# x ahead of the first scale block, low parts on VectorE, wider scale blocks: one transformer block on one core

## The chip, the core and the metric

The kernel runs on one core of a Trainium2 chip. A core has five engines, each with a queue of its own that it works through strictly in order: TensorE (PE in the profile, its weight loads PEld), VectorE (DVE), ScalarE (ACT), GpSimd (POOL) and SyncE (SP), which here issues most of the loads. An instruction waits for others by semaphores, and everything behind it on its engine waits with it. The metric is device time in microseconds (us) of one execution; lower is better.

## The reference

One decoder layer for 512 tokens of width 2048, in f32. What matters here is its head, and the MLP at its end:

```python
mod = (jax.nn.silu(c) @ w_ada[l] + b_ada[l])                 # 6 x 2048 values
shift1, scale1, gate1, shift2, scale2, gate2 = ...
h = rms_norm(x, norm1_w[l]) * (1.0 + scale1) + shift1
proj = h @ w_in[l]                                           # 2048 x 7168
...                                                          # attention, HGRN2, w_out, residual
h2 = rms_norm(x, norm2_w[l]) * (1.0 + scale2) + shift2
ff = jnp.square(jax.nn.relu(h2 @ w_ff1[l])) @ w_ff2[l]
x = x + gate2 * ff
```

## The kernel before

Every f32 product is computed as three fast ones: an operand is split into a high part, a cast (`hi`, `whi`, `vhi`), and a low part, the rest (`lo`, `wlo`, `vlo`), and TensorE adds high x high, high x low and low x high (`L205` to `L207` in the helper `ch_mm`). The casts run on ScalarE. The low parts of weights (`L40`) run on VectorE.

**The head.** scale1 is a product of one vector with 2048 columns of w_ada. It is not done on TensorE but by `gemv` on VectorE: for each of 16 row blocks k of w_ada a load (`araw`) and one instruction `acc = araw * sc[k] + acc` (`L127` for the first two, `L129` after), in two accumulators for even and odd k. `to_cols` then turns the sums over: TensorE transposes them (`pc`, `L149`), ScalarE adds them up along the rows (`L152`), and VectorE makes the scale columns `g1c` of them (`L167`, `L169`). A block of 256 columns of scale1 gives two columns of g1c, so it serves two row blocks k of the projection; it takes 32 instructions for 512 columns where a block of 512 takes 16 and one addition of the accumulators (`L143`).

x is loaded in 16 pieces (`xs`), squared and summed (ScalarE, VectorE), scaled by the reciprocal root, and transposed on TensorE (`ptx`) into 16 tiles `xnT[k]`. `scaled(k)` multiplies xnT[k] by g1c on ScalarE, casts `hi`, and takes `lo = xnT - hi` on GpSimd. `first_groups` runs the first 768 columns of w_in over k in pairs, six products of 128 columns with three matmuls each: 18 matmuls for one k. Before each pair of k it calls `scale_block`, which does the gemv of the next 256 columns of scale1. I call this the scale stage.

A second `first_groups` follows (the shift stage): 768 further columns with the same scaled operands, while VectorE does the gemv of shift1 (four blocks of 512), and `shifted(k)` adds the shift to hi and xnT and takes the low part on GpSimd. What the shift would have added to the columns of the first two groups is added later by another gemv over w_in (`shift_through`). Then comes a part whose TensorE order is written by hand (`project`, from `L197` on), up to the MLP.

**The border.** The second MLP product is a Strassen-like scheme of seven products (`product`, i = 1, 3, 5, 6, 7, 4, 2 at first) on halves of the weights: `part` forms a combination of raw weight tiles on VectorE where the product needs one (`L1073`, `L1077`), casts `vhi` on ScalarE and takes `vlo` on VectorE (`L1084`). There are four buffers for vhi and vlo. The product with `early` set is put at high priority; before, that is the first alone.

**What sets the order.** The program is written once, and a scheduler places each engine's instructions by a time line that it computes itself; `issue_after` and `high_priority` steer it. So an edit in one place can change the order of several engines, and the engine queues on the chip keep that order whatever the real times are.

Of the kernel before, what the change touches and what calls it, by code (L numbers as in the profile page):

```python
# [8 lines left out]
F32 = mybir.dt.float32  # L9
# [3 lines left out]
ALU = mybir.AluOpType  # L13
# [31 lines left out]
def hybrid_block(ctx, tc, x, c, positions, norm1_w, w_ada, b_ada, w_in, q_norm_w, k_norm_w,  # L45
# [3 lines left out]
    pe, dve, act, pool = nc.tensor, nc.vector, nc.scalar, nc.gpsimd  # L49
# [4 lines left out]
    win_v = w_in[0].rearrange("(k p) n -> p k n", p=P)  # L54
# [28 lines left out]
    n1c = const.tile([P, NK], F32, name="n1c")  # L83
# [49 lines left out]
    def run_all(g):  # L133
        for _ in g:
            pass
        return gemv.acc
# [17 lines left out]
    g1c = const.tile([P, NK], F32, name="g1c")  # L154
# [5 lines left out]
    def mod_cols(kind, b, dst, nw, n=512, early=False):  # L160

        for _ in gemv(ada_v, sc, kind * D + b * n, n, early):
            yield
        nb = n // P
        d = dst[:, b * nb:(b + 1) * nb]
        yield from to_cols(gemv.acc, d)
        dve.tensor_tensor(d, d, bcol[:, kind * NK + b * nb:kind * NK + (b + 1) * nb], op=ALU.add)  # L167
        if nw is not None:
            mod_cols.last = dve.scalar_tensor_tensor(d, d, 1.0, nw[:, b * nb:(b + 1) * nb], op0=ALU.add, op1=ALU.mult)  # L169
        yield  # L170
# [14 lines left out]
    def load_w(view, k0, c0, n=512, eng=None, ahead=True, raws=None):  # L185
        with tc.high_priority() if ahead else ExitStack():
            raw = wr.tile([P, 2, n], F32, name="wraw", tag="raw", bufs=4)
            nc.sync.dma_start(raw, view[:, k0:k0 + 2, c0:c0 + n])
            if raws is not None:
                raws[:] = [raw[:, 0], raw[:, 1]]  # L190
            return [_split(nc, wr, raw[:, j], n, eng if j else None) for j in range(2)]
# [49 lines left out]
    hhi, hlo, spare = [], [], []  # L241


    first_scale = mod_cols(1, 0, g1c, n1c, 256, True)
    for _ in range(8):
        next(first_scale)
    xs = [[slot("xs") for _ in range(4)] for _ in range(NT)]
    ssx = sm.tile([P, NT, 4], F32, name="ssx", bufs=1)
    rx = sm.tile([P, NT], F32, name="rx", bufs=1)
# [3 lines left out]
    for q in range(4):  # L253
        for ti in range(NT):
            jk = work("jk")
            with tc.issue_after(sc_ready.ins), tc.issue_after(sig_ready.ins):
                if q == 3 and ti % 2:
                    dve.tensor_tensor_reduce(jk, xs[ti][q], xs[ti][q], op0=ALU.mult, op1=ALU.add, scale=1.0, scalar=0.0,
                                             accum_out=ssx[:, ti, q:q + 1])
                else:  # L260
                    act.activation(jk, xs[ti][q], AF.Square, accum_out=ssx[:, ti, q:q + 1])
    dve.tensor_reduce(rx, ssx, axis=AX.X, op=ALU.add)
    rstd_of(rx, rx, NT, 1.0 / D)
    run_all(first_scale)
    second_scale = mod_cols(1, 1, g1c, n1c, 256, True)
    spare.extend(hp.tile([P, 512], F32, name="araw", tag=f"{c}{k}") for k in range(8, NK) for c in ("hi", "lo"))
    for _ in range(8):
        next(second_scale)
    xnT = []
    for q in range(4):  # L270
        for ti in range(NT):
# [12 lines left out]
    def first_groups(c_f, c_q, before, after):  # L284

        bt = [bank("prj", tag="mm") for _ in range(4)]
        bc = [bank("prc") for _ in range(2)]
        for k0 in range(0, NK, 2):
            before(k0)
            wt = load_w(win_v, k0, c_f, ahead=False)  # L290
            wc = load_w(win_v, k0, c_q, 256, None, ahead=False)
            for j in range(2):
                k = k0 + j
                ch_mm(bt, hhi[k], hlo[k], *wt[j], k == 0, k == NK - 1)
                ch_mm(bc, hhi[k], hlo[k], *wc[j], k == 0, k == NK - 1)
            after(k0)
        return bt, bc

    def scale_block(k0):
        if k0 == 0:  # L300
            run_all(second_scale)
        elif k0 < 14:
            run_all(mod_cols(1, k0 // 2 + 1, g1c, n1c, 256, True))
        for k in (k0, k0 + 1):
            scaled(k)

    def shift_start(k0):
        if k0 == 14:
# [19 lines left out]
    def scaled(k):  # L328
        for l, t in zip((hhi, hlo), pair(k)):
            l.append(t)  # L330
        act.activation(xnT[k], xnT[k], AF.Copy, scale=g1c[:, k:k + 1])
        act.copy(hhi[k], xnT[k])
        pool.tensor_tensor(hlo[k], xnT[k], hhi[k].bitcast(F32), op=ALU.subtract)

    def shifted(k):
        act.activation(hhi[k], xnT[k], AF.Identity, bias=s1c[:, k:k + 1])
        act.activation(xnT[k], xnT[k], AF.Identity, bias=s1c[:, k:k + 1])
        pool.tensor_tensor(hlo[k], xnT[k], hhi[k].bitcast(F32), op=ALU.subtract)

    bgw = []  # L340

# [534 lines left out]
    banks = project_out(0, 0, nothing)  # L876
# [210 lines left out]
    def product(i, c, w, tag, by_tile, early):  # L1087

        banks = [bank("f2", tag=tag) for _ in range(2)]
        fh, fl = operand(c, i)  # L1090

        def mm(u, whi, wlo, ts_):
            for a in range(2):
                for t in ts_:
                    ts = slice(t * P, (t + 1) * P)
                    first, end = u + a == 0, u + a == KG
                    pe.matmul(banks[t], lhsT=fh[:, u, a, ts], rhs=whi[:, a], start=first, stop=False)  # L1097
                    pe.matmul(banks[t], lhsT=fh[:, u, a, ts], rhs=wlo[:, a], start=False, stop=False)  # L1098
                    pe.matmul(banks[t], lhsT=fl[:, u, a, ts], rhs=whi[:, a], start=False, stop=end)  # L1099

        if by_tile:
            ws = [part(i, u, w) for u in range(KG)]
            for t in range(2):
                for u in range(KG):
                    mm(u, *ws[u], (t,))
        else:
            for u in range(KG):
                with tc.high_priority() if early else ExitStack():
                    ws = part(i, u, w)
                mm(u, *ws, range(2))  # L1110
        return banks
# [50 lines left out]
    for q in range(2):  # L1162
        for c in range(NC):
            now = order if q or c else first_order
            w = weights(c, q, now)
            for j, i in enumerate(now):
                banks = product(i, c, w, "bg" if j % 2 else "mm", i == 2 and c == NC - 1, q + c + j == 0)
                for t in range(2):
                    if c == 0:
                        done = act.copy(accs7[i, t], banks[t])  # L1170
                    elif c < NC - 1:
                        dve.tensor_tensor(accs7[i, t], accs7[i, t], banks[t], op=ALU.add)
                    else:
                        finish(q, i, t, banks[t])
            if c == 0:
                with tc.issue_after(done.ins):
                    residual_in(q)
# [52 lines left out]
```

## Time and profile before

| | us |
|---|---|
| three runs | 2361.02, 2366.8, 2368.55 (median 2366.8) |
| the profiled execution | 2359.59, span 2357.7, granted TensorE clock 0.995 |
| TensorE busy in the span | 2269.5 |
| VectorE, ScalarE, GpSimd busy | 1620.6, 982.8, 266.6 |

The span is what lies between the first and the last instruction of the profile; the time beside it has 1.9 us more. The views that the prediction quotes are these. The table by stage gives, for a stretch from A to B, its length, then busy us and instructions (x) of PE, PEld, DVE, ACT and POOL, then the granted clock of TensorE, the DMA engines' share, and GB/s. The view of waits says "who <- for whom: us in total, times, longest". The time line gives start, duration, engine, line, operation, output<-inputs, shape and count, and in brackets how long the engine had been idle and what ended it; neighbours of one kind are merged, so the spacing of a row of several is its length without the last tail, divided by their number. The rows by group give count | busy us, mean ns | idle before.

### The profile page before, as it was taken

To read this page: it belongs to the slowest core of one execution; us is meant where nothing else is said; L and a number is where in the kernel's file an instruction comes from. 1 tells how busy PE (TensorE), PEld (TensorE's weight loads), DVE (VectorE), ACT (ScalarE), POOL (GpSimd) and SP (SyncE) were. 2 spreads that over 40 slices of the span, in tenths; PEclk is the share of its full clock that TensorE was granted. 3 is DMA by queue.
4 is the path that set the end of the run, shared out by engine and by line. 5 is a ranking of instruction groups with operands and counts; after the bars stand their busy time and mean duration, and the time that the engine had idled before them with its cause. 6 is when DMAs were issued, how large, how long until landed. Compare 5 with 4: busy or idle time off the path is not lost.

```text
span 2357.7 us, 32278 instructions
## 1 busy us (share of the span) xinstructions
PE 2269.5 (96%) x11865; PEld 1858.7 (79%) x11865; DVE 1620.6 (69%) x2569; ACT 982.8 (42%) x1854; POOL 266.6 (11%) x336
## 2 busy tenths in 40 slices
PE   4998999999999999999999999999989999999999
PEld 3777877887778877878888888888868888888887
DVE  6999887677876565667544544444466788968878
ACT  5555434433444553447433333333334433344332
POOL 2332022000230000000000000000011111111110
PEclk9999999999999999999999999999999999999999
DMA  9798455556554266735565564555689877988784
GB/s 321 236 342 281 135 178 152 182 165 206 170 172 151 91 197 211 247 112 191 174 207 161 185 198 155 199 183 161 210 308 370 328 286 282 369 330 321 284 310 143
DMA packets 238894, 524.82 MB, mean 223 GB/s; under 512 B 17460, under 2 KB 38208, under 8 KB 238736
## 3 DMA queue, kind: packets, MB, share of 16 engines
q1 hardware_dynamic: 186800, 332.54, 43.4%
q0 software_dynamic: 47040, 180.79, 21.0%
q10 hardware_dynamic: 4896, 9.44, 1.2%
q8 instruction: 93, 1.52, 0.3%
q14 instruction: 65, 0.53, 0.1%
HBM read 455.57 MB, written 67.13 MB: 222 GB/s over the span
## 4 chain that ended last, share of the span: by engine, by line
PE 73%; DVE 11%; DMA 11%; issue 3%; ACT 1%; SPq 0%; ACTq 0%; POOL 0%; DVEq 0%; POOLq 0%
PE f L207 10%; PE f L205 10%; PE f L206 10%; PE f L1098 8%; PE f L1099 8%; PE f L1097 8%; DMA araw<-in_w_ada_dram 8%; PE prj L197 5%; PE prj L199 5%; PE prj L198 4%; DVE acc L129 4%; DVE wlo L40 2%; DMA araw<-in_w_in_dram 1%; PE po L497 1%; PE pscore L464 1%
## 5 line engine op out<-in xcount | busy, mean ns | idle before, releaser
L39 ACT CAST whi<-wraw 128x512 fp32r<-128x512 f32 (+1 forms) x560 | 338.3, 608 | 811.6 <-PE f L206 391.9
L40 DVE TENSOR_TENSOR wlo<-wraw,whi 128x512 fp32r<-128x512 f32 (+1 forms) x560 | 383.1, 688 | 404.4 <-ACT whi L39 371.4
L205 PE MATMUL f<-hi,whi 128*128 128x512 f32 x1024 | 398.9, 390 | 0.0
L207 PE MATMUL f<-hi,wlo 128*128 128x512 f32 x1024 | 398.6, 389 | 0.3 <-DVE wlo L40 0.3
L206 PE MATMUL f<-lo,whi 128*128 128x512 f32 x1024 | 398.4, 389 | 0.0
L1083 ACT CAST vhi<-raw 128x1024 fp32r<-128x1024 f32 x224 | 235.4, 1055 | 345.4 <-PE f L1099 312.3
L197 PE MATMUL prj<-whi,hi 128*128 128x512 f32 x896 | 365.5, 408 | 5.7 <-DVE x L921 4.3
L1098 PE MATMUL f<-vlo,Fh 128*128 128x512 f32 x896 | 349.6, 390 | 9.6 <-DVE vlo L1084 9.5
L199 PE MATMUL prj<-whi,lo 128*128 128x512 f32 x896 | 351.8, 393 | 2.9 <-DVE lo L237 2.8
L198 PE MATMUL prj<-wlo,hi 128*128 128x512 f32 x896 | 350.9, 392 | 0.0
L1099 PE MATMUL f<-vhi,Fl 128*128 128x512 f32 x896 | 349.3, 390 | 0.0
L1097 PE MATMUL f<-vhi,Fh 128*128 128x512 f32 x896 | 349.2, 390 | 0.0
L1084 DVE TENSOR_TENSOR vlo<-raw,vhi 128x1024 fp32r<-128x1024 f32 x224 | 271.8, 1220 | 111.3 <-ACT vhi L1083 111.0
L129 DVE SCALAR_TENSOR_TENSOR acc<-araw,sc,acc 128x512 f32<-128x512 f32 (+1 forms) x392 | 270.8, 718 | 103.9 <-DMA araw<-in_w_ada_dram 102.6
L207 PEld LDWEIGHTS f<-hi,wlo 128*128 128x128 f32 x1024 | 192.2, 188 | 40.7 <-DVE wlo L40 0.7
L206 PEld LDWEIGHTS f<-lo,whi 128*128 128x128 f32 x1024 | 192.2, 188 | 39.8
L205 PEld LDWEIGHTS f<-hi,whi 128*128 128x128 f32 x1024 | 192.2, 188 | 39.7
L1098 PEld LDWEIGHTS f<-vlo,Fh 128*128 128x128 f32 x896 | 168.6, 188 | 45.5 <-DVE vlo L1084 10.5
L197 PEld LDWEIGHTS prj<-whi,hi 128*128 128x128 f32 x896 | 169.3, 189 | 40.8 <-DVE x L921 5.2
L199 PEld LDWEIGHTS prj<-whi,lo 128*128 128x128 f32 x896 | 169.0, 189 | 40.9 <-DVE lo L237 4.2
L1097 PEld LDWEIGHTS f<-vhi,Fh 128*128 128x128 f32 x896 | 168.6, 188 | 35.2
L1099 PEld LDWEIGHTS f<-vhi,Fl 128*128 128x128 f32 x896 | 168.6, 188 | 35.0
(275 smaller groups left out, 2499.3 us busy)
## 6 DMA issues: line engine op xcount, KB each, us to landing
araw<-in_w_ada_dram SPq DMA_DIRECT2D x384, 256.0 KB, 4.2
wraw<-in_w_ff_dram SPq DMA_DIRECT2D x128, 512.0 KB, 3.7
raw<-in_w_ff_dram SPq DMA_DIRECT2D x128, 512.0 KB, 9.5
Fh<-f_hid POOLq DMA_DIRECT2D x56, 1024.0 KB, 8.4
Fl<-f_lod POOLq DMA_DIRECT2D x56, 1024.0 KB, 11.5
wraw<-in_w_in_dram SPq DMA_DIRECT2D x104, 512.0 KB, 4.0
f_hid<-fh POOLq DMA_DIRECT2D x16, 1792.0 KB, 7.4
f_lod<-fl POOLq DMA_DIRECT2D x16, 1792.0 KB, 11.8
```

Source lines behind the costliest of these rows:

```text
L39: nc.scalar.copy(hi, src)
L40: (eng or nc.vector).tensor_tensor(lo, src, hi.bitcast(F32), op=ALU.subtract)
L129: dve.scalar_tensor_tensor(acc, raw[:, k - k0], vec[:, k:k + 1], acc, op0=ALU.mult, op1=ALU.add)
L197: pe.matmul(banks[ti], lhsT=hi[:, ts], rhs=whi, start=first, stop=False)
L198: pe.matmul(banks[ti], lhsT=hi[:, ts], rhs=wlo, start=False, stop=False)
L199: pe.matmul(banks[ti], lhsT=lo[:, ts], rhs=whi, start=False, stop=last)
L205: pe.matmul(banks[j], lhsT=whi[:, js], rhs=hi, start=first, stop=False)
L206: pe.matmul(banks[j], lhsT=whi[:, js], rhs=lo, start=False, stop=False)
L207: pe.matmul(banks[j], lhsT=wlo[:, js], rhs=hi, start=False, stop=last)
L1097: pe.matmul(banks[t], lhsT=fh[:, u, a, ts], rhs=whi[:, a], start=first, stop=False)
L1098: pe.matmul(banks[t], lhsT=fh[:, u, a, ts], rhs=wlo[:, a], start=False, stop=False)
L1099: pe.matmul(banks[t], lhsT=fl[:, u, a, ts], rhs=whi[:, a], start=False, stop=end)
```

## The change

Four edits, all but the last in the head. The 16 loads of x are issued before those of the first scale block, whose gemv is placed behind the last square on VectorE; eight of the 16 squares run on VectorE in place of two, and the first two weight loads stand ahead of the sum. The low parts of `scaled` and `shifted` move from GpSimd to VectorE. After two blocks of 256 columns the scale comes in three blocks of 512, and each block's gemv is placed behind the last low part of the pair before it. At the border the first two products are `early`, not the first alone.

```diff
     first_scale = mod_cols(1, 0, g1c, n1c, 256, True)
-    for _ in range(8):
-        next(first_scale)
     xs = [[slot("xs") for _ in range(4)] for _ in range(NT)]
...
-                if q == 3 and ti % 2:
-                    dve.tensor_tensor_reduce(jk, xs[ti][q], xs[ti][q], op0=ALU.mult, op1=ALU.add, scale=1.0, scalar=0.0,
-                                             accum_out=ssx[:, ti, q:q + 1])
+                if ti % 2:
+                    squared = dve.tensor_tensor_reduce(jk, xs[ti][q], xs[ti][q], op0=ALU.mult, op1=ALU.add, scale=1.0, scalar=0.0,
+                                                       accum_out=ssx[:, ti, q:q + 1])
                 else:
                     act.activation(jk, xs[ti][q], AF.Square, accum_out=ssx[:, ti, q:q + 1])
+    with tc.issue_after(squared.ins):
+        for _ in range(8):
+            next(first_scale)
+    first_w = [load_w(win_v, 0, 4096, ahead=False), load_w(win_v, 0, 3072, 256, None, ahead=False)]
...
-    second_scale = mod_cols(1, 1, g1c, n1c, 256, True)
...
-    for _ in range(8):
-        next(second_scale)
...
     def scale_block(k0):
-        if k0 == 0:
-            run_all(second_scale)
-        elif k0 < 14:
-            run_all(mod_cols(1, k0 // 2 + 1, g1c, n1c, 256, True))
         for k in (k0, k0 + 1):
-            scaled(k)
+            done = scaled(k)
+        with tc.issue_after(done.ins):
+            if k0 == 0:
+                run_all(mod_cols(1, 1, g1c, n1c, 256, True))
+            elif k0 in (2, 6, 10):
+                run_all(mod_cols(1, (k0 + 2) // 4, g1c, n1c, 512, True))
...
-        pool.tensor_tensor(hlo[k], xnT[k], hhi[k].bitcast(F32), op=ALU.subtract)
+        return dve.tensor_tensor(hlo[k], xnT[k], hhi[k].bitcast(F32), op=ALU.subtract)
...
-        pool.tensor_tensor(hlo[k], xnT[k], hhi[k].bitcast(F32), op=ALU.subtract)
+        dve.tensor_tensor(hlo[k], xnT[k], hhi[k].bitcast(F32), op=ALU.subtract)
...
-                banks = product(i, c, w, "bg" if j % 2 else "mm", i == 2 and c == NC - 1, q + c + j == 0)
+                banks = product(i, c, w, "bg" if j % 2 else "mm", i == 2 and c == NC - 1, q + c == 0 and j < 2)
```

The line numbers of the new kernel are 1 to 3 lower or higher than before (`L279` becomes `L278`, `L1084` becomes `L1087`). The four places of the order that the prediction uses follow. Names are those of the tiles; a number behind a name tells two tiles of one name apart.

TensorE at the very start, before: the transposes of the first block's sums (pc), those of x (ptx), the first products (prj).

```order
L82 MATMUL ps_c<-ident,crow 128x128
L149 MATMUL pc<-ident,acc 128x128 x4
L279 MATMUL ptx<-ident,xs 128x128 x32
L205 MATMUL prj<-hi_473,whi 128x512 x4
L279 MATMUL ptx<-ident,xs 128x128 x4
```

And now:

```order
L82 MATMUL ps_c<-ident,crow 128x128
L149 MATMUL pc<-ident,acc 128x128
L278 MATMUL ptx<-ident,xs 128x128 x12
L149 MATMUL pc<-ident,acc 128x128 x3
L278 MATMUL ptx<-ident,xs 128x128 x32
L205 MATMUL prj<-hi_458,whi 128x512 x4
```

One transpose of block 0's sums still stands first, and x's stand behind it; the sums themselves are now made after x has come.

VectorE between x and the scale of block 0, now (before, block 0 and its g1c stood ahead of the squares):

```order
L264 TENSOR_REDUCE rx<-ssx 128x4
L129 SCALAR_TENSOR_TENSOR acc<-araw,sc,acc 128x256 x2
L210 TENSOR_SCALAR rx<-rx 128x4
L129 SCALAR_TENSOR_TENSOR acc<-araw,sc,acc 128x256 x4
L274 TENSOR_SCALAR xs<-xs,rx 128x512 x3
L129 SCALAR_TENSOR_TENSOR acc<-araw,sc,acc 128x256
L274 TENSOR_SCALAR xs<-xs,rx 128x512 x4
L129 SCALAR_TENSOR_TENSOR acc<-araw,sc,acc 128x256
L274 TENSOR_SCALAR xs<-xs,rx 128x512 x7
L129 SCALAR_TENSOR_TENSOR acc<-araw,sc,acc 128x256 x2
L40 TENSOR_TENSOR wlo<-wraw,whi 128x512 x2
L40 TENSOR_TENSOR wlo<-wraw,whi 128x256 x2
```

Four more `L129` and then the g1c of block 0 follow: the scalings of x and the first weight splits stand inside the block.

VectorE around one scale block in the middle of the scale stage, before (one pair of k):

```order
L127 TENSOR_SCALAR acc<-araw,sc 128x256 x2
L40 TENSOR_TENSOR wlo<-wraw,whi 128x256
L129 SCALAR_TENSOR_TENSOR acc<-araw,sc,acc 128x256 x4
L40 TENSOR_TENSOR wlo<-wraw,whi 128x256
L129 SCALAR_TENSOR_TENSOR acc<-araw,sc,acc 128x256 x2
L167 TENSOR_TENSOR g1c<-g1c,bcol 128x2
L129 SCALAR_TENSOR_TENSOR acc<-araw,sc,acc 128x256 x3
L169 SCALAR_TENSOR_TENSOR g1c<-g1c,n1c 128x2
L129 SCALAR_TENSOR_TENSOR acc<-araw,sc,acc 128x256 x2
```

And now (four k: the end of the first block of 512 and the start of the second):

```order
L129 SCALAR_TENSOR_TENSOR acc<-araw,sc,acc 128x512 x5
L143 TENSOR_TENSOR acc<-acc 128x512
L167 TENSOR_TENSOR g1c<-g1c,bcol 128x4
L169 SCALAR_TENSOR_TENSOR g1c<-g1c,n1c 128x4
L336 TENSOR_TENSOR lo_660<-xnT,hi_659 128x512
L336 TENSOR_TENSOR lo_665<-xnT,hi_664 128x512
L336 TENSOR_TENSOR lo_726<-xnT,hi_725 128x512
L336 TENSOR_TENSOR lo_731<-xnT,hi_730 128x512
L127 TENSOR_SCALAR acc<-araw,sc 128x512 x2
L129 SCALAR_TENSOR_TENSOR acc<-araw,sc,acc 128x512 x6
```

Before, g1c stood among the parts of the next block; now the next block begins behind the four low parts.

ScalarE at the same place, now (whi is the cast of weights, two of 512 and two of 256 columns for a pair of k):

```order
L334 ACTIVATE xnT<-xnT,g1c 128x512 x4
L335 CAST hi_659<-xnT 128x512
L335 CAST hi_664<-xnT 128x512
L335 CAST hi_725<-xnT 128x512
L335 CAST hi_730<-xnT 128x512
L39 CAST whi<-wraw 128x512 x2
L39 CAST whi<-wraw 128x256 x2
L39 CAST whi<-wraw 128x512 x2
L39 CAST whi<-wraw 128x256 x2
L152 ACTIVATE pc,g1c<-pc 128x128 x4
```

The eight casts of the next two pairs of k stand ahead of the next block's reads of pc; before, the reads of pc stood two casts behind each pair's hi.

VectorE at the border, before: combinations of raw weights (L1073, L1077), then the first split of the second product.

```order
L1073 TENSOR_TENSOR raw_15582<-raw_15598,raw_15582 128x1024
L1077 TENSOR_TENSOR raw_15598<-raw_15590,raw_15598 128x1024
L1084 TENSOR_TENSOR vlo<-raw_15586,vhi 128x1024
L1073 TENSOR_TENSOR raw_15584<-raw_15600,raw_15584 128x1024
L1084 TENSOR_TENSOR vlo<-raw_15588,vhi 128x1024
L1077 TENSOR_TENSOR raw_15600<-raw_15592,raw_15600 128x1024
```

And now:

```order
L1076 TENSOR_TENSOR raw_15510<-raw_15526,raw_15510 128x1024
L1080 TENSOR_TENSOR raw_15526<-raw_15518,raw_15526 128x1024
L1087 TENSOR_TENSOR vlo<-raw_15514,vhi 128x1024
L1076 TENSOR_TENSOR raw_15512<-raw_15528,raw_15512 128x1024
L1080 TENSOR_TENSOR raw_15528<-raw_15520,raw_15528 128x1024
L1087 TENSOR_TENSOR vlo<-raw_15516,vhi 128x1024
```

Both pieces are preceded by the same four combinations; the first split keeps its place behind six, and the second moves behind one more.

More of the change, by code (lines that the diff above doesn't have):

```diff
@@ L289, in first_groups @@
             before(k0)
-            wt = load_w(win_v, k0, c_f, ahead=False)
-            wc = load_w(win_v, k0, c_q, 256, None, ahead=False)
+            if first_w:
+                wt, wc = first_w.pop(0), first_w.pop(0)
+            else:
+                wt = load_w(win_v, k0, c_f, ahead=False)
+                wc = load_w(win_v, k0, c_q, 256, None, ahead=False)
             for j in range(2):
```

## The prediction

> **What bounds the kernel now.** I read the page first, then the busy time by stage, then the waits of the first 250 us.
>
> ```profile
> PE 2269.5 (96%) x11865; PEld 1858.7 (79%) x11865; DVE 1620.6 (69%) x2569; ACT 982.8 (42%) x1854; POOL 266.6 (11%) x336
> ...
> 1100.00:1700.00 600.00, 600.00 (x2649) 496.82 (x2648) 279.14 (x364) 214.70 (x306) 28.09 (x30) 1.00 0.57 184
> ...
> 37.66:53.60 15.94, 13.55 (x76) 10.91 (x76) 15.94 (x37) 12.12 (x29) 2.92 (x2) 1.00 1.07 360
> 53.60:63.62 10.02, 8.97 (x41) 7.10 (x41) 10.02 (x20) 5.08 (x11) 8.02 (x3) 1.00 1.10 354
> 63.62:84.18 20.56, 18.38 (x84) 14.20 (x82) 20.56 (x48) 9.09 (x23) 4.79 (x4) 1.00 0.97 312
> 84.18:105.16 20.98, 18.55 (x81) 14.30 (x81) 20.98 (x43) 10.17 (x25) 6.43 (x4) 1.00 0.72 239
> 105.16:123.50 18.34, 17.84 (x75) 13.75 (x76) 15.95 (x46) 11.62 (x26) 6.42 (x4) 1.00 0.30 88
> 123.50:203.20 79.70, 70.73 (x305) 55.76 (x303) 74.54 (x115) 38.83 (x94) 27.51 (x20) 0.98 0.90 311
> ...
> ACT xnT L331 <- DVE g1c L169: 23.3, 7, 4.9
> ...
> PE ptx L279 <- ACT xs L273: 12.7, 1, 12.7
> PE pc L149 <- DVE acc L129: 12.4, 1, 12.4
> ...
> PE prj L205 <- ACT hi L332: 7.4, 7, 2.4
> ```
>
> TensorE is busy 96% of the span; where nothing holds it, it issues 2649 products in 600 us, 0.227 us each. The rows by stage (times from the span's start; busy PE, PEld, DVE, ACT, POOL) begin where TensorE takes row blocks k = 0, 2, 4, 8 and 12 of the first projection, then the shift stage, which ends at 203.20. VectorE is busy every microsecond from 37.66 to 105.16, so it paces this stage, about 21 us for four row blocks in which TensorE needs 72 x 0.227 = 16.3. Everything the diff moves, save the border, lies ahead of 203.20, and from there the order of all engines is nearly that of before: a shift of that moment is carried to the end.
>
> **x first.**
>
> ```profile
> 25.08 0.69 DVE L258 CUSTOM_DVE_ANT_0 jk<-xs 128x512 f32<-128x512 f32 x1 [4.96 <-DMA xs<-in_x_dram]
> ...
> 30.36 6.41 PE L279 MATMUL ptx<-ident,xs 128*128 128x128 f32 x32 [12.67 <-ACT xs L273]
> 37.66 0.50 PE L205 MATMUL prj<-hi,whi 128*128 128x512 f32 x1 [0.90 <-ACT hi L332]
> ...
> 33.71 2.46 DVE L275 TENSOR_SCALAR xs<-xs,rx 128x512 f32<-128x512 f32 x6
> 42.33 0.75 DVE L40 TENSOR_TENSOR wlo<-wraw,whi 128x256 fp32r<-128x256 f32 x2
> 65.31 0.68 DVE L40 TENSOR_TENSOR wlo<-wraw,whi 128x512 fp32r<-128x512 f32 x1
> 65.91 1.66 DVE L129 SCALAR_TENSOR_TENSOR acc<-araw,sc,acc 128x256 f32<-128x256 f32 x4
> ```
>
> The last part of x landed at 25.1 behind 8 scale loads of 256 KB. At the 355 GB/s of these rows the 2.1 MB take 5.9 us, so x now ends at 19.2. Six more squares on VectorE (0.69 each) fall into the arrival, where it idled; the reciprocal root is ready near 22. But SP's queue has swapped two loads, not shortened: scale, x and the first weights still end together. And TensorE's order now has one transpose of the scale's sum (pc) ahead of all transposes of x. It needs all 16 parts of block 0, and VectorE's order puts behind x's arrival, one after the other: 14 L129 at 0.40, 2 L127 at 0.30, 14 scalings of x at 0.41 and four weight splits (2 x 0.60, 2 x 0.33): 5.6 + 0.6 + 5.7 + 1.9 = 13.8, from 20.2 to 34.0. Only then TensorE starts on x, 3.6 us later than the 30.36 of before. From there ScalarE's order has 3 copies, 2 pc reads, 2 copies, 2 scalings, 2 copies and the cast hi ahead of the first product, near 7 us at 0.52 to 0.62 each: first product at 41.0, before 37.66. The head loses 3.3 us instead of gaining 5.9; bounds -3 (ScalarE's copies overlap worse before) and +6.
>
> **Low parts on VectorE.**
>
> ```profile
> 62.45 2.94 DVE L129 SCALAR_TENSOR_TENSOR acc<-araw,sc,acc 128x256 f32<-128x256 f32 x2
> 67.83 0.86 DVE L129 SCALAR_TENSOR_TENSOR acc<-araw,sc,acc 128x256 f32<-128x256 f32 x2
> ...
> L333 POOL TENSOR_TENSOR lo<-xnT,hi 128x512 fp32r<-128x512 f32 x16 | 28.6, 1803 | 59.3 <-ACT hi L332 51.8 <-DVE acc L129 7.4
> L338 POOL TENSOR_TENSOR lo<-xnT,hi 128x512 fp32r<-128x512 f32 x12 | 24.2, 2047 | 41.9 <-ACT xnT L337 28.0 <-ACT whi L39 14.0
> ...
> 204.91 2.73 DVE L129 SCALAR_TENSOR_TENSOR acc<-araw,s1c,acc 128x512 f32<-128x512 f32 x4
> 207.67 0.69 DVE L143 TENSOR_TENSOR acc<-acc 128x512 f32<-128x512 f32 x1
> ```
>
> While GpSimd computes a low part, VectorE stalls: the same two L129 take 2.94 instead of 0.86 us, 1.04 per low part. On VectorE one costs what L143 of that shape costs, 0.60 from start to start. So each of the 32 moved saves VectorE 0.44, if nothing makes it wait. **Blocks of 512**: 16 L129 at 0.664 plus one L143 instead of 32 at 0.40 save 1.5 us per four row blocks.
>
> **What the order adds.** VectorE now has nothing between a block's last L129 and its low parts but the scale itself, and each of these needs ScalarE. Before, seven to eight L129 of the next blocks stood there.
>
> ```profile
> 180.35 0.26 ACT L152 ACTIVATE pc<-pc 128x128 f32<-128x128 f32 x1 [3.81 <-PE pc L149]
> ...
> 181.72 0.19 ACT L152 ACTIVATION_READ_ACCUMULATOR pc<-pc 128x1 f32 x1
> ...
> 71.32 1.34 ACT L331 ACTIVATE xnT<-xnT,g1c 128x512 f32<-128x512 f32 x2 [4.29 <-DVE g1c L169]
> ...
> 73.07 1.14 ACT L332 CAST hi<-xnT 128x512 fp32r<-128x512 f32 x2
> ...
> 105.16 1.20 PE L205 MATMUL prj<-hi,whi 128*128 128x512 f32 x4 [1.09 <-ACT hi L332]
> ...
> 203.20 0.39 PE L197 MATMUL prj<-whi,hi 128*128 128x512 f32 x1
> ```
>
> For a block of 512: TensorE's four transposes (0.7 to ScalarE's start), four pc reads (180.35 to 181.91, 1.6), the two g1c instructions (0.35): 2.7 us. Then four scalings at 0.62 and the first cast hi, 0.65: 3.2 us until the first low part and the first product can start. VectorE waits through both, 5.9 us, and so does TensorE, whose order has the block's products behind its pc. VectorE's work for a block is 10.1 (two L127 at 0.40, 14 L129) + 0.6 + 8 weight splits 3.7 + 4 low parts 2.4 + 0.3 = 17.1; with 5.9 of waits 23.0, against 21 before. Worse, nothing is done ahead any more. By this sum, from the first product at 41.0: the low parts of k = 0, 1 are done by 43, the 16 parts of block 1 (256 columns) and one weight split by 49.5; there TensorE's order holds 12 products (2.7) behind the block's first pc, and behind them come the last weight cast, two pc reads, scale, two scalings and hi, 4.1 in all: k = 2 near 56.5 (53.60 before). Low parts to 57.8, 12.7 of work, 2 of waiting for weight casts that need TensorE, 5.9: k = 4 at 78.3 (63.62). Low parts to 80.8; ScalarE now casts k = 8's weights ahead of the pc reads and needs TensorE's products of k = 4 to 7 done, 78.3 + 16.3 + 1.7 (clock, below) = 96.3; last cast and reads 2.2, scale 0.35, 3.2: k = 8 at 102.1 (84.18). Low parts to 104.5, 14.4 of work, and 12 L127 and L129 of the shift between (7.4): L143 ends at 125.0 (two of the L129 stand behind it), + 5.9: k = 12 at 130.9, before 105.16. That is 26 us behind.
>
> **What comes back.** From k = 12 to 203.20 lie 360 products, 81.7 us alone; before they took 98.0. In the shift stage VectorE's work, counted from the order behind the tables of rotations, is 53 L129, 10 L127, 3 L143, 12 low parts and 14 pairs of splits: 35.2 + 4.0 + 1.8 + 7.2 + 13.1 = 61.3; before, 58 L129, 4 L143 and 12 x 1.04 of stalls made it 71.
>
> ```profile
> 127.28 1.48 DVE L129 SCALAR_TENSOR_TENSOR acc<-araw,sc,acc 128x512 f32<-128x512 f32 x2 [0.67 <-DMA araw<-in_w_ada_dram]
> ```
>
> VectorE resumes the shift 3.8 us after 123.5, behind loads that SP issues after six weight loads; SP's order is the same, and I take 5. So 130.9 + 16.3 (k = 12 to 15) + 1.7 + 5 + 61.3 + 2.8 (last products) = 218.0, 15 us after 203.2. The shift stage takes 69.1 of that; its bounds are 66 (TensorE alone) and the 79.7 of before, -3 and +11. One microsecond more for the five L129 that now stand behind: +16.
>
> **Border.**
>
> ```profile
> 1742.79 1.23 DVE L1073 TENSOR_TENSOR raw<-raw,raw 128x1024 f32<-128x1024 f32 x1 [1.66 <-DMA raw<-in_w_ff_dram]
> ...
> 1751.95 0.79 PE L1098 MATMUL f<-vlo,Fh 128*128 128x512 f32 x1 [9.55 <-DVE vlo L1084]
> ...
> 1752.00:1755.00 3.00, 3.00 (x7) 2.42 (x8) 3.00 (x3) 0.00 (x0) 0.00 (x0) 0.50 1.04 369
> 1755.00:1760.00 5.00, 5.00 (x22) 4.04 (x22) 4.97 (x5) 1.81 (x2) 0.00 (x0) 0.93 1.00 377
> ```
>
> The 9.55 us gap comes from six combinations of raw weights, each waiting for loads, ahead of the second product's first split. In the new order the same six stand ahead of it; only the second split moves behind one more. I cost it at 0 (bounds -1 and +1).
>
> After that gap the granted clock was 0.50 for 3 us: 7 products instead of 13, 1.4 to 1.7 us. The new gaps (13, 6 and 11 us ahead of k = 4, 8, 12) should cost the same; two of them lie on the path, as taken. [...]
>
> **Sum.** +16 on the profiled execution's 2359.6 (span 2357.7 and 1.9 around it). That lies 7.2 under the median 2366.8 of the runs shown, so I put it on the median: 2383.
>
> **Rivals.** Faster: VectorE's waits do not appear, because work stands in them after all. Its plain work to the last g1c is then 78.8 us from 19.9 (28 and 52 L129, 12 low parts, 14 pairs of splits), k = 12 comes at 102, and with the shorter shift stage the change gains 15: 2352. For it speaks that VectorE is 100% busy before and that GpSimd's stalls go; against it, the order. It decides when less than half of the 29 us between 102 and 131 is waited. Same: just about half of them, 2367. [...] The border split does move ahead of the combinations, against the order: -10 on top, 2373.
>
> **Chances.** Forecast 0.66 (own range 2372 to 2391), slower still 0.14, same 0.09, faster 0.08, border 0.03. A measurement of this kernel tells 0.3%, 7 us, from no change. So slower 0.83, same 0.09, faster 0.08. The range takes in the 29 us down to a half on one side, and the shift stage as before on the other: 2366 to 2397.
>
> **What would show it.** TensorE's first transposes of x wait behind acc, near 34; L205 of k = 0 near 41; VectorE idle 2 to 3 us twice per block, released by ACT pc and ACT hi; PE L205 waiting for ACT hi near 30 us in all, 7.4 before; no 1.5 us L129 in the first 200 us; L197 starting near 219; the border gap still 9 to 10 us with VectorE's six combinations before it. It is wrong if VectorE is still full from 41 on, or if L197 starts before 203.

## The result, and the profile after

| | before | after |
|---|---|---|
| median of six runs each | 2364.39 us | 2385.15 us |
| ratio | | 1.0086, 95% interval 1.0067 to 1.0104 |
| profiled execution's span | 2357.7 us | 2384.3 us |
| granted TensorE clock | 0.995 | 0.986 |

The change costs 20.8 us, 0.9%. The page first: GpSimd is busy 58.6 us less, VectorE has less to do too, and TensorE, which does the same products and twelve transposes of sums fewer (`L149`, 116 for 128), is busy 4.7 us longer.

```profile
PE 2274.2 (95%) x11853; PEld 1866.7 (78%) x11853; DVE 1610.4 (68%) x2562; ACT 982.2 (41%) x1842; POOL 208.0 (9%) x304
```

The table by stage has the same columns as before (length; busy us and instructions of PE, PEld, DVE, ACT, POOL; granted clock; DMA share; GB/s). Its rows begin where TensorE takes row blocks k = 0, 2, 4, 8 and 12, and end at the first `L197`; the last two are stretches just behind two gaps.

```profile
43.30:58.77 15.47, 11.52 (x62) 9.07 (x61) 9.94 (x25) 10.12 (x23) 0.00 (x0) 1.00 0.93 333
58.77:80.04 21.27, 11.17 (x40) 8.52 (x40) 14.43 (x26) 7.11 (x19) 0.00 (x0) 0.77 0.42 136
80.04:104.15 24.11, 18.96 (x77) 15.30 (x77) 17.52 (x32) 10.22 (x25) 0.00 (x0) 0.85 0.72 240
104.15:134.22 30.07, 19.97 (x78) 15.85 (x78) 27.24 (x61) 10.21 (x25) 0.00 (x0) 0.78 0.53 174
134.22:217.90 83.68, 83.67 (x365) 68.71 (x365) 72.32 (x143) 46.27 (x102) 2.74 (x8) 0.97 0.84 299
...
59.90:63.30 3.40, 3.40 (x10) 2.59 (x9) 3.40 (x7) 0.00 (x0) 0.00 (x0) 0.54 0.00 0
...
80.00:84.00 4.00, 3.96 (x9) 3.14 (x10) 3.98 (x8) 1.55 (x3) 0.00 (x0) 0.50 0.03 4
```

VectorE, 100% busy in this stage before, is busy 9.94 of 15.47, 14.43 of 21.27 and 17.52 of 24.11 us. Behind the gaps the clock is one half (0.54 and 0.50). The time line of TensorE and VectorE shows the rhythm of a block:

```profile
34.76 0.48 PE L149 MATMUL pc<-ident,acc 128*128 128x128 f32 x1 [30.60 <-DVE acc L129]
...
58.77 1.20 PE L205 MATMUL prj<-hi,whi 128*128 128x512 f32 x4 [3.40 <-ACT hi L335]
...
76.53 0.16 DVE L167 TENSOR_TENSOR g1c<-g1c,bcol 128x4 f32<-128x4 f32 x1 [2.86 <-ACT pc L152]
80.02 2.50 DVE L336 TENSOR_TENSOR lo<-xnT,hi 128x512 fp32r<-128x512 f32 x4 [3.13 <-ACT hi L335]
80.04 2.07 PE L205 MATMUL prj<-hi,whi 128*128 128x512 f32 x4 [5.15 <-ACT hi L335]
...
100.64 0.16 DVE L167 TENSOR_TENSOR g1c<-g1c,bcol 128x4 f32<-128x4 f32 x1 [1.40 <-ACT pc L152]
104.13 2.50 DVE L336 TENSOR_TENSOR lo<-xnT,hi 128x512 fp32r<-128x512 f32 x4 [3.13 <-ACT hi L335]
104.15 2.07 PE L205 MATMUL prj<-hi,whi 128*128 128x512 f32 x4 [5.15 <-ACT hi L335]
...
134.22 2.08 PE L205 MATMUL prj<-hi,whi 128*128 128x512 f32 x4 [2.71 <-ACT hi L335]
```

VectorE stands twice per block: once from its last sum until ScalarE has read the turned sums (76.53), once until the first `hi` is there (80.02). TensorE starts within 0.02 us of VectorE, since both waited for the same cast; its first four products then take 2.07 us where they took 1.20. The waits of the first 230 us, summed ("who <- for whom: us, times, longest"):

```profile
PE prj L205 <- ACT hi L335: 16.4, 4, 5.1
DVE lo L336 <- ACT hi L335: 12.7, 6, 3.5
DVE g1c L167 <- ACT pc L152: 10.9, 5, 4.4
PE pc L149 <- DVE acc L143: 10.4, 2, 5.4
```

The hand-ordered part begins 14.7 us later than before (`L197`, 203.2 then). As a second mark I use the first matmul into the tile `pA` (256.3 before): behind it the order of TensorE is the same in all kernels here.

```profile
L197 PE MATMUL prj<-whi,hi x48: 389/389/776, 217.9 to 259.5; 128*128 128x512 f32 x48
```

```profile
L573 PE MATMUL pA<-z x768: 196/196/217, 277.3 to 693.6; 128*32 128x32 f32 x192
```

At `pA` the loss is 21.0 us, as much as the medians differ. (The two profiled spans lie 26.6 us apart: the profiled execution of before is 4.8 us below its median, that of after 1.0 above.) At the border, the gap before the second product grew a little; combinations of raw weights stand ahead of its split and wait for loads, 2.23 us here.

```profile
1767.95 1.23 DVE L1076 TENSOR_TENSOR raw<-raw,raw 128x1024 f32<-128x1024 f32 x1 [2.23 <-DMA raw<-in_w_ff_dram]
...
1777.97 0.80 PE L1101 MATMUL f<-vlo,Fh 128*128 128x512 f32 x1 [10.97 <-DVE vlo L1087]
```

### The profile page after: what moved, and what is told of

Read it like the earlier page. It is cut to its first block, busy times and chain, and to the rows that moved or that the text cites. A ratio compares the mean times of both kernels' runs of the same rounds, so it can differ in the third digit from the quotient of the medians.

```text
span 2384.3 us, 32152 instructions
## 1 busy us (share of the span) xinstructions
PE 2274.2 (95%) x11853; PEld 1866.7 (78%) x11853; DVE 1610.4 (68%) x2562; ACT 982.2 (41%) x1842; POOL 208.0 (9%) x304
## 4 chain that ended last, share of the span: by engine, by line
PE 80%; DVE 8%; DMA 8%; ACT 2%; issue 2%; SPq 0%; DVEq 0%; ACTq 0%
PE f L207 10%; PE f L205 10%; PE f L206 10%; PE f L1101 8%; PE f L1102 8%; PE f L1100 8%; DMA araw<-in_w_ada_dram 6%; PE prj L197 5%; PE prj L199 5%; PE prj L198 5%; DVE acc L129 2%; PE prj L205 2%; PE prj L206 2%; PE prj L207 2%; DVE wlo L40 1%
## 5 line engine op out<-in xcount | busy, mean ns | idle before, releaser
L40 DVE TENSOR_TENSOR wlo<-wraw,whi 128x512 fp32r<-128x512 f32 (+1 forms) x560 | 376.4, 676 | 418.9 <-ACT whi L39 386.4
L197 PE MATMUL prj<-whi,hi 128*128 128x512 f32 x896 | 367.1, 410 | 5.1 <-DVE x L924 3.7
L1087 DVE TENSOR_TENSOR vlo<-raw,vhi 128x1024 fp32r<-128x1024 f32 x224 | 272.8, 1225 | 111.5 <-ACT vhi L1086 111.2
L129 DVE SCALAR_TENSOR_TENSOR acc<-araw,sc,acc 128x512 f32<-128x512 f32 (+1 forms) x350 | 246.5, 730 | 99.0 <-DMA araw<-in_w_ada_dram 98.1
L197 PEld LDWEIGHTS prj<-whi,hi 128*128 128x128 f32 x896 | 170.3, 190 | 41.0 <-DVE x L924 4.6
```

The costliest lines, as they stand in the source:

```text
L40: (eng or nc.vector).tensor_tensor(lo, src, hi.bitcast(F32), op=ALU.subtract)
L129: dve.scalar_tensor_tensor(acc, raw[:, k - k0], vec[:, k:k + 1], acc, op0=ALU.mult, op1=ALU.add)
L197: pe.matmul(banks[ti], lhsT=hi[:, ts], rhs=whi, start=first, stop=False)
```

## The experiments

Each ratio is to the kernel before, run in turn on the same chip; 0.001 is 2.4 us. `L197` and `pA` are the starts in the profiled execution. The three kernels below that differ from before at the border alone have `L197` at 201.2 to 202.2 and `pA` at 255.9 to 257.0, so two executions of one head differ by some 2 us at the first mark and 1 us at the second.

| kernel | ratio (95%) | L197 | pA |
|---|---|---|---|
| before | 1 | 203.2 | 256.3 |
| after | 1.0086 (1.0067 to 1.0104) | 217.9 | 277.3 |
| after, gemv placed freely | 0.9980 (0.9969 to 0.9990) | 193.0 | 252.4 |
| after, gemv behind g1c | 1.0036 (1.0025 to 1.0047) | 204.6 | 264.0 |
| before + low parts | 0.9958 (0.9945 to 0.9970) | 187.0 | 246.6 |
| before + low parts + placement | 1.0091 (1.0077 to 1.0104) | 218.2 | 278.7 |
| before + low parts + blocks of 512 | 0.9959 (0.9944 to 0.9973) | 186.6 | 246.4 |
| before + x first | 1.0018 (1.0008 to 1.0027) | 205.4 | 260.1 |
| before + border edit | 1.0004 (0.9991 to 1.0017) | 201.2 | 255.9 |
| before + border's splits first | 0.9999 (0.9987 to 1.0010) | 201.5 | 256.2 |
| before + splits first + residual spread | 0.9959 (0.9946 to 0.9973) | 202.2 | 257.0 |
| before + low parts + splits first | 0.9963 (0.9952 to 0.9975) | 187.0 | 246.6 |
| before + low parts + splits first + residual spread | 0.9914 (0.9898 to 0.9930) | 187.5 | 247.3 |

**The placement taken away.**

```diff
         for k in (k0, k0 + 1):
-            done = scaled(k)
-        with tc.issue_after(done.ins):
-            if k0 == 0:
+            scaled(k)
+        if k0 == 0:
...
```

> The changed kernel with one thing undone: the gemv of the next scale block is no longer placed behind the low part of the pair before it. Head, low parts on VectorE, blocks of 512 and border stay as changed. Theory (the placement costs the time): in the new order the parts of the blocks 1 and 2 stand among those of block 0, so the first product comes later than 43.3, near 49; after that VectorE has work through every pc and hi, its 2.9 and 3.1 us waits per block shrink below 1 us, k = 12 starts near 105 (134.2 in the changed kernel), L197 between 190 and 205 (217.9), and the time is 2352 to 2366. Rival (blocks of 512 or low parts on VectorE cost the time themselves): L197 stays near 218 and the time near 2385. Rival (the head costs it): the time stays above 2378.

Measured: 2356.1 us against 2361.0 for before. First product, the stage from there to the third gap, the waits, and `L197`, each of its own view:

```profile
48.38 1.48 PE L205 MATMUL prj<-hi,whi 128*128 128x512 f32 x4 [1.93 <-ACT hi L335]
```

```profile
48.38:92.51 44.13, 38.70 (x152) 30.68 (x152) 42.93 (x78) 21.83 (x55) 0.00 (x0) 0.88 0.98 344
```

```profile
PE prj L205 <- ACT hi L335: 7.4, 3, 3.2
...
DVE g1c L167 <- ACT pc L152: 0.6, 1, 0.6
...
DVE lo L336 <- ACT hi L335: 0.4, 1, 0.4
```

```profile
L197 PE MATMUL prj<-whi,hi x81: 389/389/775, 193.0 to 259.5; 128*128 128x512 f32 x81
```

VectorE's two waits have gone (0.6 and 0.4 us in all, 10.9 and 12.7 in the changed kernel), VectorE is full again (42.93 of 44.13 us), and although the first product starts 5 us later than in the changed kernel, `L197` starts 24.9 us sooner. The placement alone costs 0.0106, 25 us: more than the whole loss. Blocks of 512, the low parts and the head stand as changed in this kernel, so none of them is to blame for it. TensorE's waits for hi go from 16.4 to 7.4 us, the longest 3.2.

**The low parts alone, and with the placement.** The first kernel is before with `dve` in place of `pool` in `scaled` and `shifted`; the second has in addition (blocks of 256, old head):

```diff
     def scale_block(k0):
-        if k0 == 0:
-            run_all(second_scale)
-        elif k0 < 14:
-            run_all(mod_cols(1, k0 // 2 + 1, g1c, n1c, 256, True))
         for k in (k0, k0 + 1):
-            scaled(k)
+            done = scaled(k)
+        with tc.issue_after(done.ins):
+            if k0 == 0:
+                run_all(second_scale)
+            elif k0 < 14:
+                run_all(mod_cols(1, k0 // 2 + 1, g1c, n1c, 256, True))
```

> The kernel before with one part of the change: the 32 low parts of scaled and shifted on VectorE. Theory: each saves VectorE 0.44 us where VectorE paces, so k = 12 comes 5 us earlier than 105.16, L197 near 193 (203.2), time 2354 to 2358. Rival (a low part on VectorE makes it wait for ScalarE's hi and costs more than the stall it removes): VectorE idles behind ACT hi, L197 at 203 or later, time 2364 or above.

> As the run with the low parts alone, and in addition the placement: the gemv of the next scale block behind the last low part of the pair before it (blocks of 256, head of before). Theory: from k = 4 on VectorE waits near 1.9 us for pc and 1.9 for hi per pair, 14 us per pair in place of 10; k = 12 near 122, L197 near 212, time 2368 to 2385, some 18 us above the low parts alone. Rival (the placement is harmless, the new head or the blocks of 512 are to blame): within 4 us of the low parts alone.

Measured: 2351.1 and 2382.6 us. The low parts alone gain 9.9 us, more than the 3 to 7 that I expected, and `L197` comes at 187.0 where I expected 193. In the first 260 us the sums of the scale cost VectorE (group of `L129`, count | busy, mean ns | idle before), first in the kernel before, then with the low parts on VectorE:

```profile
L129 DVE SCALAR_TENSOR_TENSOR acc<-araw,sc,acc 128x256 f32<-128x256 f32 (+1 forms) x171 | 108.5, 675 | 6.6 <-DMA araw<-in_w_ada_dram 6.4
```

```profile
L129 DVE SCALAR_TENSOR_TENSOR acc<-araw,sc,acc 128x256 f32<-128x256 f32 (+1 forms) x171 | 90.5, 566 | 2.2 <-DMA araw<-in_w_ada_dram 2.0
...
L333 DVE TENSOR_TENSOR lo<-xnT,hi 128x512 fp32r<-128x512 f32 x16 | 10.6, 677 | 0.0
```

The same 171 sums take 18.0 us less, and on the page of this run VectorE's busy time is 1608.3 in place of 1620.6, although it does 32 instructions more: 0.38 us less per low part (I had taken 0.44). With the placement the gain turns into a loss of 31.5 us against the low parts alone. The second kernel's time line has the gaps, one per pair of k, all alike (two more follow, at 107.27 and 120.92):

```profile
64.33 2.08 PE L205 MATMUL prj<-hi,whi 128*128 128x512 f32 x4 [3.33 <-ACT hi L333]
...
78.94 1.49 PE L205 MATMUL prj<-hi,whi 128*128 128x512 f32 x4 [3.33 <-ACT hi L333]
...
93.59 2.08 PE L205 MATMUL prj<-hi,whi 128*128 128x512 f32 x4 [3.34 <-ACT hi L333]
```

The period is 13.7 to 14.7 us per pair (I had expected 14), and in it VectorE is busy 9.8. `L197` came at 218.2 where I expected 212, and the loss is 31.5 us where I expected some 18. So the placement costs 25 us in the one surrounding and 31 in the other, without the new head and without blocks of 512.

**The placement one step earlier.** The changed kernel, with the next block behind the scale columns of this one:

```diff
+        columns = mod_cols.last
         for k in (k0, k0 + 1):
-            done = scaled(k)
-        with tc.issue_after(done.ins):
+            scaled(k)
+        with tc.issue_after(columns.ins):
```

> The changed kernel, with the gemv of the next scale block placed behind the columns g1c of this block in place of its last low part: 3 to 9 L129 of the next block then stand between g1c and the first low part, but nothing stands between L143 and g1c. Theory (both waits cost VectorE's time one for one): the 12.7 us in which low parts wait for hi go, the 10.9 us for pc stay, L197 moves from 217.9 to near 206, and the time is 10 to 15 us below the changed kernel, 1.002 to 1.005 of before. Rival (only the wait for pc counts, since TensorE cannot start before hi in any case): within 5 us of the changed kernel.

Measured: 2369.6 us, ratio 1.0036; that is 12 us below the changed kernel's ratio. The low parts hardly wait for hi any more, while TensorE and the scale columns wait nearly as before:

```profile
PE prj L205 <- ACT hi L336: 11.2, 3, 5.2
DVE g1c L167 <- ACT pc L152: 10.5, 5, 4.4
...
DVE lo L337 <- ACT hi L336: 0.4, 2, 0.2
```

The 12.3 us that went from VectorE's queue came back as 13.3 at both marks. The gaps of TensorE are still up to 5.2 us long, so those do not set the time of this stage; VectorE's lost time does. The rest above the free placement, 0.0056 or 13 us, goes with the wait for pc: VectorE spends 10.5 us in it here and 0.6 with free placement. No run takes that wait away alone.

**x first, alone.** The new head on the kernel before (16 loads of x ahead of the first block, eight squares on VectorE, first weights ahead of the sum), everything else as before.

> The kernel before with the new head alone: x ahead of the first scale block, eight squares on VectorE, first two weight loads ahead of the sum. Blocks of 256, low parts on GpSimd, gemv placed freely. In its order the parts of blocks 1 and 2 stand ahead of block 0's scale. Theory (VectorE paces the stage, so what counts is how much of its work is done, not when the first product starts): first product late, near 49, but k = 12 near 105 as before and the time 2360 to 2370. Rival (the head costs what it delays the first product): k = 12 near 115 and the time 2375 or more. Rival (x earlier helps): below 2357.

Measured: 2365.9 against 2361.0 us, 1.0018.

```profile
35.63 0.48 PE L149 MATMUL pc<-ident,acc 128*128 128x128 f32 x1 [31.45 <-DVE acc L129]
...
48.31 1.20 PE L205 MATMUL prj<-hi,whi 128*128 128x512 f32 x4 [0.84 <-ACT hi L337]
```

TensorE waits 31 us for the first transpose of the sums, and the first product starts 10.6 us later than before; but k = 12 starts at 107.62 (105.16 before), and `L197` comes only 2.2 and `pA` 3.8 us late. The new head is a small loss, not a gain, and it is not the start of the first product that measures it. Its three edits were not run apart.

**Blocks of 512, alone on top of the low parts.**

```diff
-        elif k0 < 14:
-            run_all(mod_cols(1, k0 // 2 + 1, g1c, n1c, 256, True))
+        elif k0 in (2, 6, 10):
+            run_all(mod_cols(1, (k0 + 2) // 4, g1c, n1c, 512, True))
```

> The kernel with the low parts alone on VectorE, and in addition scale blocks of 512 from the third on, gemv placed freely. Theory: 32 L129 of 256 at 0.40 become 16 of 512 at 0.66 and one L143, 1.5 us less of VectorE per block, so the time is 3 to 5 us below the low parts alone (0.9958 of before), 0.994. Rival (a block of 512 comes late as a whole, since its first two row blocks wait for all four columns): 3 us or more above the low parts alone.

Measured: 0.9959, next to 0.9958 with blocks of 256: no difference that can be told, with intervals that reach some 3 us to either side; `L197` and `pA` are within 0.4 us as well. Why the 3 to 5 us did not come stays open. Two gaps of TensorE may be where they went, though no run proves it (the kernel with the low parts alone has one of 4.06 too, at 94.31): the products of k = 2 wait 4.06 us for hi, and the transposes of the first wide block 4.58 for its sum.

```profile
53.45 2.08 PE L205 MATMUL prj<-hi,whi 128*128 128x512 f32 x4 [4.06 <-ACT hi L332]
68.55 1.09 PE L149 MATMUL pc<-ident,acc 128*128 128x128 f32 x4 [4.58 <-DVE acc L143]
```

**The border edit alone.** `q + c == 0 and j < 2` on the kernel before.

> The kernel before with the border edit alone: the first two products of the second MLP product at high priority, not the first alone. Theory: in the order the same six combinations stay ahead of the first split of the second product, so the gap stays between 9 and 11 us and the time within 3 us of before. Rival (the edit brings the splits forward): gap below 3 us and 8 to 11 us less time.

Measured: 1.0004, the gap is 9.70 us:

```profile
1755.14 0.80 PE L1098 MATMUL f<-vlo,Fh 128*128 128x512 f32 x1 [9.70 <-DVE vlo L1084]
```

As its order said, the edit does nothing. **The gap itself** is a matter of order, and can be closed:

```diff
         if i == 5:
-            dve.tensor_tensor(b11, b12, b11, op=ALU.subtract)
+            with tc.issue_after(last_split_of_second_product.ins):   # the first time
+                dve.tensor_tensor(b11, b12, b11, op=ALU.subtract)
```

> The kernel before with one new edit at the border: the first combinations of the third product in line (i = 5) are placed behind the last split of the second (i = 3), so VectorE's order has the four splits ahead of all combinations. Theory: the 9.55 us gap was VectorE's order, so it shrinks below 2 us, the 3 us of half clock behind it go, and the time is 8 to 11 us below before. Rival (the loads of the raw weights set the end there): the wait comes back ahead of the third product, and the time is at most 4 us below before.

> Both: low parts on VectorE and the four splits of the second product ahead of the combinations, the rest as before. Theory: the two lie 1500 us apart and add up: 0.9958 of before less another 8 to 11 us, 0.991 to 0.993. Rival: what the border gains stays out, as for the run with that edit alone.

Measured: 0.9999 and 0.9963, nothing gained in either. In the first of the two, the gap at the border has shrunk to 1.49 us, and another stands 70 us behind it (TensorE, then ScalarE with its queue ACTq, in the kernel with the splits first):

```profile
1822.26 0.79 PE L1104 MATMUL f<-vhi,Fh 128*128 128x512 f32 x1 [7.14 <-ACT vhi L1088]
```

```profile
1807.38 13.75 ACTq L1134 DMA_DIRECT2D d<-x1d  x8
1821.17 3.89 ACT L1088 CAST vhi<-raw 128x1024 fp32r<-128x1024 f32 x4 [13.58 <-DMA d<-x1d]
```

In the kernel before the same eight issues stand at the same place of the queue:

```profile
1819.45 5.66 ACTq L1127 DMA_DIRECT2D d<-x1d  x8
1825.15 3.90 ACT L1083 CAST vhi<-raw 128x1024 fp32r<-128x1024 f32 x4 [5.49 <-issue]
```

ScalarE issues eight residual loads of 256 KB in one go, and its next casts stand behind them. Earlier in time the DMA engines are still full with weights (a share of 1.04 during the issues, 0.83 before), the issues take 13.75 in place of 5.66 us, and TensorE runs out of `vhi`. The second kernel shows less of it: its issues take 8.23 us, the gap at the border is 2.10 us and the one behind only 1.62 (8.96 and none with the low parts alone). There the profile names a raw weight as the last thing that the cast waited for; it lands at 1813.00, and the issues end at 1813.90:

```profile
1813.94 3.89 ACT L1088 CAST vhi<-raw 128x1024 fp32r<-128x1024 f32 x4 [8.06 <-DMA raw<-in_w_ff_dram]
```

So the rival was right that the gain is given back. In the first kernel ScalarE's queue ends the wait, by the profile; in the second the cast could have started at most 0.9 us sooner without the issues, so late weights hold it too. That execution, 2348.4 us, is also the fastest of its seven (median 2351.1), so its short gaps don't show where the gain of the others went. The loads were then spread over two groups of products:

```diff
-            if c == 0:
-                with tc.issue_after(done.ins):
-                    residual_in(q)
+                if c in (1, 2):                      # behind each product
+                    if c == 1 and j == 0:
+                        loads = residual_in(q)       # now a generator, one load each
+                    with tc.issue_after(last_vhi_cast.ins):
+                        next(loads, None)
```

> Low parts on VectorE and the border's splits first, and in addition the nine loads of gate and residual (which ScalarE issued in one go behind the first group of seven products, 13.75 us of its queue in the run with the border's splits first, with the next vhi behind them) issued one by one, each behind the last vhi cast of a product in the two groups after. Theory: what the border gained was lost again to that stretch of ScalarE's queue; without it the 7.1 us gap near 1822 goes, and the time is 7 to 10 us below the low parts alone: 0.9915 to 0.993 of before. Rival (the DMA engines are full from 1731 to 1800, so the raw weights come late in any case): a gap of the same size stays, 0.995 to 0.997.

> As the first run of this group, with the low parts on GpSimd as before: the two border edits alone. Theory: 7 to 10 us below before, 0.996 to 0.997, and the two gains add up. Rival: same as before, 0.999 to 1.001, as for the splits alone.

Measured: 2341.6 us (0.9914) with the low parts and 2350.5 (0.9959) without. In the first, TensorE's longest gap near the border is 1.44 us, and the stage behind it is full at full clock:

```profile
1745.88 0.50 PE L1105 MATMUL f<-vlo,Fh 128*128 128x512 f32 x1 [1.44 <-DVE vlo L1089]
```

```profile
1740.00:1800.00 60.00, 58.17 (x256) 47.52 (x255) 44.29 (x39) 28.59 (x34) 7.46 (x10) 1.00 1.04 388
1800.00:1850.00 50.00, 50.00 (x222) 41.43 (x221) 42.05 (x41) 20.07 (x20) 7.45 (x10) 1.00 0.88 317
```

The two gains add up (0.0042 + 0.0041 against 0.0086). Spreading the loads is thus what lets the border's gain through. Since it frees ScalarE's queue and also takes those bytes from the stretch in which the DMA engines are full (a share of 1.02 to 1.04 from 1731 to 1800 with the splits first), the runs don't say which of the two it is. This kernel is 20 us faster than before and 41 us faster than the changed one, by the ratios.

## Why the prediction was right, and where its steps were off

The forecast was 2383 in a range of 2366 to 2397; the changed kernel takes 2385.15. The step from before to after is 20.8 us by the medians, where the sum had 16; the median of before over all six runs lies 2.4 us under that of the three that the forecast stood on. So the step was forecast 4.8 us too small, and that the level came out within 2 us is in part luck.

- **The main cause was named and is shown.** The parts add up: low parts -0.0042, x first +0.0018, border +0.0004, blocks of 512 0.0001 make 0.9981, and the changed kernel with a free placement measures 0.9980 (each of these is known to 0.001 or so). What is left to 1.0086 is the placement. Free placement was the rival called faster (2352 if VectorE's waits do not appear): with the waits gone it takes 2356.
- **The cycle of a block** was close: k = 4 to 8 took 24.1 us (23.8 forecast), k = 2 to 4 21.3 (21.8), k = 8 to 12 30.1 (28.8). The wait for hi was 3.13 (3.2). The wait for pc was 2.86 once, then 1.40 and 1.48 (2.7): in the second block part of it appears at the weight splits ahead, which wait for their casts (0.81 and 0.93), and in the third two `L129` of the shift stand inside it.
- **The head** was forecast at 3.3 us, and alone it costs 0.0018, 4.3 us. The reason given does not hold: it was read from when the first product starts (41.0 forecast, 43.4 measured). In the head alone that start is 10.6 us late and the cost still 4. Where VectorE paces, only its own lost time counts.
- **The clock** was put on the path twice, 1.7 us each, from the 0.50 for 3 us behind the border's gap before. In the changed kernel it fell to one half behind five gaps of the first 250 us (0.50 to 0.54 over 3.4 us behind each), the 3.40 us ahead of k = 2 among them (0.54 in 59.90 to 63.30), which the sum had left out. In the head it stays at 1.00 (34.70 to 38.00, behind 30.60 us of waiting). How much of the half clock lies on the path the runs do not separate. The upper end of the range, 2397, and "slower still" in the chances take 3.4 us more for the clock beside the 10.6 for a shift stage as long as before: no run shows that 3.4, and in its place the runs showed the clock at 0.54 behind the gap ahead of k = 2 and at 1.00 in the head.
- **The shift stage** came on time by two errors: k = 12 3.3 us late (134.2 for 130.9), the stage 83.7 long (87.1 forecast). A part of that is not saved: eight products of the first projections stand behind the first `L197` and none before, and four more transposes.
- **"One more for the five L129 that stand behind"** was the step that was off most. From `L197` to `pA` another 6.3 us are lost (14.7 becomes 21.0). The transposes of the last shift block wait 4.84 us for its sum, 2.60 before, the clock falls behind that wait (0.51 in 244.40 to 247.80; the four take 1.07 us, 0.66 before), and the products and transposes left behind take a part of the rest. The placement is not the reason: from `L197` to `pA` all eight kernels with the low parts on VectorE take 59.4 to 60.5 us, the low parts alone 59.6 with the same wait (4.85), and the five with them on GpSimd 53.1 to 54.8. So this loss came with the low parts (whose net gain at `pA` is 9.7 us even so), and `L197` was not the mark at which the sum could stop.

```profile
244.41 1.07 PE L149 MATMUL pc<-ident,acc 128*128 128x128 f32 x4 [4.84 <-DVE acc L143]
```

- **The border** was costed at 0 and measures 0.0004 alone; in the profiled execution after, its gap is 1.4 us longer (10.97, where 9 to 10 was the sign).
- **Signs.** VectorE idle twice per block (for hi 3.13 us, for pc less than 2 from the second wide block on), the first pc near 34 (34.76), `L197` near 219 (217.9), no `L129` of 1.5 us (the longest of the first 200 us is 0.767) held. The 30 us of TensorE's waits for hi did not: 16.4 stand there and 15.2 at transposes that wait for sums (10.4 up to 230). It is one delay, and the trace books it on the instruction that stands first in the queue.

## What to carry to other kernels

On an engine that paces a stage, work of the next block is what fills the waits of this one; placing it behind this block's last step turns its waits for other engines into lost time, here 25 to 31 us for a change that moved no work at all. Count the pacing engine's idle time, not the start of the first product. And when a gap is closed, look for the next queue that the same transfers pass: here a gain of 10 us came only once ScalarE no longer issued its loads in one go ahead of its casts.

## What the runs showed of the hardware

- In the kernel with low parts and placement, TensorE's clock fell behind each of the five gaps of 3.33 us, to 0.50 to 0.61 over the 3.4 us behind. Only four transposes stand there between the gap and the last product, so the pause between products was 3.77 us or longer. The stretches behind three of them, with the clock in the column behind the five engines:

```profile
64.30:67.70 3.40, 3.37 (x8) 2.69 (x9) 3.38 (x9) 0.50 (x1) 0.00 (x0) 0.50 0.12 30
78.90:82.30 3.40, 3.37 (x9) 2.65 (x10) 3.38 (x9) 0.50 (x1) 0.00 (x0) 0.61 0.13 27
93.60:97.00 3.40, 3.40 (x9) 2.69 (x10) 3.40 (x9) 0.45 (x1) 0.00 (x0) 0.54 0.15 34
```

  In the changed kernel, the clock was still full in the first microsecond behind the gap that ends at 58.77 (1.00 in 58.80 to 59.80, four products in 1.20 us) and fell only then (0.54 in 59.90 to 63.30). The runs don't show why. The length of a gap alone does not decide: behind 2.38 us the clock of before stayed at 1.00 (53.60 to 57.00), behind 2.19 us in the kernel with the free placement it was 0.65 (92.50 to 95.90).
- ScalarE's time to issue the same eight loads was 5.66 us at a DMA share of 0.83 and 13.75 us at 1.04; what stands behind them in its queue waits that long. Three more traces point the same way: 4.64 and 5.50 us at 0.85 and 0.88 (changed kernel, low parts alone), 8.23 at 1.03 (low parts and splits first). The share alone does not set the time. First the kernel with the splits first, then before:

```profile
1807.40:1821.10 13.70, 7.72 (x35) 6.06 (x33) 3.38 (x3) 0.19 (x1) 1.13 (x2) 0.87 1.04 388
```

```profile
1819.40:1825.10 5.70, 5.70 (x27) 4.72 (x26) 3.46 (x3) 0.27 (x1) 1.20 (x2) 1.00 0.83 272
```
